# Seven-product down projection, re-shared low parts of weights and attention in pieces of one k-tile

## The chip, the cores and the metric

The kernel runs on one NeuronCore of a Trainium2 chip. The metric is the device time of one execution in microseconds. The engines are TensorE (PE in the profile; its weight loads are PEld), VectorE (DVE), ScalarE (ACT), GpSimd (POOL) and SyncE (SP, which issues most DMAs). "Low part" and "high part" are the two halves into which a float32 operand is split for an fp32r product.

## The reference

One layer of a hybrid encoder block on 512 tokens of width 1024, in float32:

```python
h = rms_norm(x, norm1_pre)
q, k, v, z, xbc, dt_raw, gates = split_cols(h @ w_in, ...)
q, k = rope(head_rms_norm(q)), rope(head_rms_norm(k))        # 8 q heads, 2 kv heads, width 64
attn_out = softmax(q k^T / 8) v @ w_attn_proj
ssd_out = ssd_branch(z, xbc, dt_raw, ...) @ w_ssd_proj       # conv, two scans, gate by silu(z)
mixed = (sigmoid(g_attn) * attn_out + sigmoid(g_ssd) * ssd_out) @ w_out
x = x + rms_norm(mixed, norm1_post)
h2 = rms_norm(x, norm2_pre)
ffn = (silu(h2 @ w_gate) * (h2 @ w_up)) @ w_down             # D_FF = 2816 = 22 k-tiles of 128
x = x + rms_norm(ffn, norm2_post)
```

## The kernel before

Every large product is made of three fp32r products (mm3, L176 to L179): low activation by high weight, high by low, high by high, accumulated in one PSUM bank of 128x512. Matrices are cut into k-tiles of 128.

Weights stream through `weights`, `wload`, `presplit` and `wnext` (L101 to L150): SP loads a raw tile, ACT casts the high part, and a letter says who makes the low part: "v" a DVE subtraction, "g" a Pool subtraction, "d" an ACT multiplication by -1 and then a DMA from Pool's queue that adds the weight from memory onto it (L145). Three buffers of raw and four each of the high and low part are in flight.

The stages come in this order. `setup` forms h transposed (hT) and q; `kvproj` makes k and v; `xbc` makes the 12 channel blocks of the conv input, on an order written out by hand for all four compute engines: after each half block the table `inner` places transposes of k, q and x, and after each block `tasks` places one step of the rope and the head norm of k and q (`krope`, `qrope`, `head_norm`). `attention` then goes over the 8 heads, with softmax rows, four transposes of 128x128 for each k-tile (L654) and, after every second head, the eight value products of both heads (L678), each 64 output rows. Its order is set by `weave`: main and fill work each yield an estimate in us, and fill (`zproj` for w_z, then `gates` for w_g) is traced when its share falls behind. Within that the scheduler of the framework orders each engine. `decays` runs in between.

The feed-forward stage has PE in an order by hand. `ffn` makes three blocks j of gate and up plainly (`prepare_plain`, slots of 512 columns with tag "t"), the first two on the first 256 tokens while the mixing steps (`combine`) of token tiles 2 and 3 still run, and the other 19 by a scheme of seven products. `down` multiplies the 22 activation tiles by w_dn in `token_major8`: all eight PSUM banks, 18 k-tiles bank by bank, the last four k-tiles by token tile so that a token tile's epilogue can start while PE works on the next. Low parts are DVE's here.

## Time and profile before

| what | value |
|---|---|
| three timed runs, median | 851.0 us (847.55 to 851.08) |
| profiled execution | 855.7 us, of it span 853.8 us |
| PE busy | 822.2 us, 4570 matmuls |
| DVE busy | 550.2 us |
| ACT busy | 434.2 us |
| POOL busy | 178.7 us |
| moved by DMA | 120.88 MB |

A busy PE is not a PE at its peak: starts of neighbouring matmuls, the list of waits and the granted clock of a stretch show where time is lost inside the busy share.

### The profile page before, as it was taken

The numbers are of one execution on the slowest core, as the hardware profiler recorded it, in microseconds if no ns is written. First come the engines' busy times: TensorE is split into PE (matmuls) and PEld (weight loads), VectorE is DVE, ScalarE is ACT, GpSimd is POOL, SyncE is SP. The second block draws the span as 40 slices with busy tenths as digits, with TensorE's granted clock in tenths as the row PEclk, the third lists the DMA queues.
The fourth block names the chain that finished last, engine by engine and source line by source line (L and its number), as shares of the span: only waits on it lengthen the run. The fifth ranks groups of instructions, "written<-read, shape, count | busy, mean of one in ns | idle before, by whom it ended". The sixth has DMA issues, their size and how long they took to land.

```text
span 853.8 us, 12071 instructions
## 1 busy us (share of the span) xinstructions
PE 822.2 (96%) x4570; PEld 689.6 (81%) x4570; DVE 550.2 (64%) x918; ACT 434.2 (51%) x775; POOL 178.7 (21%) x142
## 2 busy tenths in 40 slices
PE   8989899899899999999999989999999999999996
PEld 7768787666666777767888788999999999888885
DVE  3958884965325545676683796788788788533326
ACT  6656585554664434157333655555555556322222
POOL 3323122310113334539551011000000100000000
PEclk9989999999999999999999999999999999999999
DMA  9586551110676665137335542677666674522314
GB/s 309 173 210 146 118 142 51 50 50 0 149 175 145 162 147 137 62 111 221 124 124 196 174 124 72 183 190 196 187 186 175 174 182 151 182 94 95 99 50 148
DMA packets 42826, 120.88 MB, mean 142 GB/s; under 512 B 5264, under 2 KB 5648, under 8 KB 42768
## 3 DMA queue, kind: packets, MB, share of 16 engines
q1 hardware_dynamic: 36000, 95.46, 32.7%
q0 software_dynamic: 6768, 24.64, 16.9%
q8 instruction: 36, 0.59, 0.3%
q14 instruction: 22, 0.18, 0.1%
HBM read 111.70 MB, written 8.39 MB: 141 GB/s over the span
## 4 chain that ended last, share of the span: by engine, by line
PE 78%; DVE 9%; DMA 4%; issue 4%; ACT 3%; POOL 2%; SPq 0%; DVEq 0%; POOLq 0%; ACTq 0%
PE sa L973 10%; PE mm L177 8%; PE mm L178 8%; PE mm L179 8%; PE sc L973 6%; PE mm L973 3%; PE sb L973 3%; PE sc L177 3%; PE sc L179 3%; PE sc L178 3%; PE sa L178 2%; PE sa L179 2%; PE sa L177 2%; PE sc L678 2%; PE sb L177 2%
## 5 line engine op out<-in xcount | busy, mean ns | idle before, releaser
L142 ACT CAST whi<-raw 128x1024 fp32r<-128x1024 f32 (+3 forms) x85 | 85.0, 1003 | 56.1 <-PE sc L179 49.3
L147 POOL TENSOR_TENSOR wlo<-raw,whi 128x1024 fp32r<-128x1024 f32 (+3 forms) x31 | 65.1, 2105 | 93.5 <-ACT whi L142 91.3
L177 PE MATMUL mm<-hT,wlo 128*128 128x512 f32 x176 | 74.7, 425 | 6.5 <-DMA wlo<-in_w_xbc 4.1
L179 PE MATMUL mm<-hT,whi 128*128 128x512 f32 x176 | 70.3, 400 | 0.0
L178 PE MATMUL mm<-hT,whi 128*128 128x512 f32 x176 | 69.9, 397 | 0.0
L147 DVE TENSOR_TENSOR wlo<-raw,whi 128x1024 fp32r<-128x1024 f32 (+1 forms) x26 | 31.7, 1218 | 53.3 <-ACT whi L142 53.3
L1016 POOL DMA_DIRECT2D raw<-in_w_gu x19 | 16.4, 864 | 219.0 <-DVE wlo L1022 60.6
L1021 ACT CAST whi<-raw 128x512 fp32r<-128x512 f32 (+1 forms) x57 | 41.6, 762 | 36.3 <-PE mm L973 15.5
L1022 DVE TENSOR_TENSOR wlo<-raw,whi 128x512 fp32r<-128x512 f32 (+1 forms) x57 | 47.7, 866 | 18.5 <-ACT whi L1021 18.4
L973 PE MATMUL sa<-R,whi 128*128 128x256 f32 x304 | 56.4, 283 | 0.0
L177 PEld LDWEIGHTS mm<-hT,wlo 128*128 128x128 f32 x176 | 33.8, 192 | 17.0 <-ACT wlo L144 4.7
L973 PEld LDWEIGHTS sa<-R,whi 128*128 128x128 f32 x304 | 47.4, 192 | 0.0
L973 PE MATMUL sa<-R,wlo 128*128 128x256 f32 x152 | 43.0, 283 | 0.0
L144 ACT ACTIVATE wlo<-raw 128x1024 fp32r<-128x1024 f32 x28 | 29.7, 1060 | 25.2 <-PE mm L177 24.3
L178 PEld LDWEIGHTS mm<-hT,whi 128*128 128x128 f32 x176 | 33.8, 192 | 8.9 <-issue 2.4
L179 PEld LDWEIGHTS mm<-hT,whi 128*128 128x128 f32 x176 | 33.7, 192 | 7.8 <-issue 0.5
L145 POOL DMA_DIRECT2D wlo<-in_w_g x16 | 14.0, 872 | 108.2 <-ACT wlo L144 58.4
L639 DVE TENSOR_REDUCE nmax<-sa 128x1 f32<-128x512 f32 x32 | 21.6, 686 | 16.2 <-PE sa L637 15.9
L973 PE MATMUL sa<-h2T,b 128*128 128x256 f32 x228 | 30.5, 283 | 0.0
L1124 DVE TENSOR_TENSOR acl<-act,ach 128x512 fp32r<-128x512 f32 x22 | 14.9, 688 | 23.3 <-ACT ach L1123 23.3
L973 PEld LDWEIGHTS sa<-R,wlo 128*128 128x128 f32 x152 | 29.2, 192 | 0.1
L973 PEld LDWEIGHTS sa<-h2T,b 128*128 128x128 f32 x228 | 28.7, 192 | 0.0
(439 smaller groups left out, 2476.5 us busy)
## 6 DMA issues: line engine op xcount, KB each, us to landing
raw<-in_w_gu SPq DMA_DIRECT2D x44, 512.0 KB, 4.6
raw<-in_w_dn SPq DMA_DIRECT2D x22, 512.0 KB, 3.5
raw<-in_w_gu POOLq DMA_DIRECT2D x19, 512.0 KB, 5.3
raw<-in_w_g SPq DMA_DIRECT2D x16, 512.0 KB, 6.0
wlo<-in_w_g POOLq DMA_DIRECT2D x16, 512.0 KB, 6.7
raw<-in_w_xbc SPq DMA_DIRECT2D x12, 512.0 KB, 4.2
wlo<-in_w_xbc POOLq DMA_DIRECT2D x12, 512.0 KB, 8.0
b<-in_w_gu SPq DMA_DIRECT2D x19, 256.0 KB, 5.5
```

The costliest lines, as they stand in the source:

```text
L142: self.A.copy(h[:, :n], raw[:, :n])
L144: self.A.mul(l[:, :n], raw[:, :n], -1.0)
L147: e.tensor_tensor(l[:, :n], raw[:, :n], h[:, :n].bitcast(F32), ALU.subtract)
L177: self.T.matmul(o, ll, rh, start=first, stop=False)
L178: self.T.matmul(o, lh, rl, start=False, stop=False)
L179: self.last_mm = self.T.matmul(o, lh, rh, start=False, stop=last)
L639: V.tensor_reduce(nmax, ps, AX.X, ALU.max, negate=True)
L678: self.T.matmul(po[i * HD : i * HD + HD, :], self.vt[:, k, g * HD : g * HD + HD], pts[h - 1 + i][k], start=k == 0, stop=k == NT - 1)
L973: self.T.matmul(dst, x, y[:, k], start=start and k == 0 and i == 0, stop=k == 3 and i == 2, skip_group_check=True)
L1016: G.dma_start(p13, wgu[:, 1:3], accum_op=ALU.add)
L1021: A.copy(dst[0], src)
L1022: lo.tensor_tensor(dst[1], src, dst[0].bitcast(F32), ALU.subtract)
```

## The change

Five things change.

The down projection: the first 6 of the 22 k-tiles stay plain, the first two of them started while the last gate/up block is finished (`down_start`). The other 16 become a 2x2 block product (8 k-tiles by 256 tokens by 512 columns a block) in Strassen-Winograd form, seven products in place of eight. Sums of weight blocks are formed in memory tiles `ch` and `p3` by accumulating DMAs from Pool's queue, sums of activations by DVE, and each product's parts are added from PSUM into eight tiles `c`. PE's order by hand now covers the down projection too. New pools "la" and "lq" hold its tiles; five activation tiles move to tiles that are free by then.

Low parts of weights: kv chunks 2 and 3 from Pool to DMA, w_xbc blocks 0 to 2 from DMA to Pool, the second half of w_z from Pool to DMA.

Attention and its fill are traced in pieces of one k-tile; the value products of a k-tile are issued for both heads together, after the transposes of that k-tile.

Head norm and k: q's multiplication goes to Pool, all copies of transposed k to ACT, and the second half of k's transposes half a block later. The diagonal of row scales is made in one DVE step instead of four.

The start of the feed-forward stage: combine(2) and combine(3) are issued after the last low part of h2T; the third plain block uses tiles of 1024 columns.

The low parts on Pool's queue: before, at the kv chunks and the first blocks of w_xbc:

```order
L147 TENSOR_TENSOR wlo_367<-raw_137,whi_366 128x864
L147 TENSOR_TENSOR wlo_379<-raw_139,whi_378 128x576
L145 DMA wlo_440<-in_w_xbc 128x1024
L145 DMA wlo_447<-in_w_xbc 128x1024
L145 DMA wlo_579<-in_w_xbc 128x1024
```

after, at the same place:

```order
L147 DMA wlo_364<-in_w_kv 128x864
L147 DMA wlo_377<-in_w_kv 128x576
L149 TENSOR_TENSOR wlo_439<-raw_436,whi_438 128x1024
L149 TENSOR_TENSOR wlo_445<-raw_442,whi_444 128x1024
L149 TENSOR_TENSOR wlo_576<-raw_573,whi_575 128x1024
L147 DMA wlo_582<-in_w_xbc 128x1024
```

The kv subtractions (864 and 576 columns) have become DMAs, the first three w_xbc DMAs subtractions of 1024 columns.

PE at one group of value products (pt is a transposed probability tile, vt is v, mm the fill's bank); before, the first pair of heads:

```order
L654 MATMUL sb_1602<-cst_100,pr_1448 128x128
L678 MATMUL sc_1622<-pt_1586,vt_451 64x512
L678 MATMUL sc_1622<-pt_1479,vt_451 64x512
L678 MATMUL sc_1622<-pt_1593,vt_451 64x512
L678 MATMUL sc_1622<-pt_1486,vt_451 64x512
L678 MATMUL sc_1622<-pt_1600,vt_451 64x512
L678 MATMUL sc_1622<-pt_1493,vt_451 64x512
L678 MATMUL sc_1622<-pt_1607,vt_451 64x512
L178 MATMUL mm_1609<-wlo_1241,hT_345 128x512
L179 MATMUL mm_1609<-whi_1240,hT_345 128x512
```

after, the second pair of heads:

```order
L178 MATMUL mm_1845<-whi_1698,hT_343 128x512
L179 MATMUL mm_1845<-wlo_1699,hT_341 128x512
L180 MATMUL mm_1845<-whi_1698,hT_341 128x512
L678 MATMUL sc_1823<-pt_1746,vt_448 64x512
L678 MATMUL sc_1823<-pt_1854,vt_448 64x512
L178 MATMUL mm_1845<-whi_1705,hT_344 128x512
L179 MATMUL mm_1845<-wlo_1706,hT_342 128x512
L180 MATMUL mm_1845<-whi_1705,hT_342 128x512
L678 MATMUL sc_1823<-pt_1756,vt_448 64x512
L678 MATMUL sc_1823<-pt_1869,vt_448 64x512
L178 MATMUL mm_1845<-whi_1705,hT_344 128x512
```

Before, the products of four k-tiles stand in one row with a lone one at an end; after, two stand together for each k-tile with fill between.

DVE at the start of the feed-forward stage (L162 before and L164 after write the row scale; R and af are the mixing step's); before:

```order
L932 TENSOR_TENSOR R_1075_4537<-mm_4420,R_1074_4536 128x512
L192 RECIPROCAL ry_4521<-rt_4522 128x4
L933 SCALAR_TENSOR_TENSOR R_1074_4536<-R_1075_4537,af_4174 128x512
L206 TENSOR_TENSOR rt_4522<-ry_4521 128x4
L935 SCALAR_TENSOR_TENSOR af_4176<-R_1074_4536,af_4176 128x512
L207 TENSOR_TENSOR rt_4522<-rt_4522,rn_4520 128x4
L208 SCALAR_TENSOR_TENSOR ry_4521<-rt_4522,ry_4521 128x4
L162 COPY rstd_142<-ry_4521 128x4
L183 TENSOR_TENSOR h2T_3918<-sc_4503,h2T_3916 128x4x128
L183 TENSOR_TENSOR h2T_3919<-sc_4504,h2T_3917 128x4x128
L165 TENSOR_SCALAR diag_4530<-cst_100,rstd_142 128x128 x4
```

after:

```order
L164 COPY rstd_142<-ry_4526 128x4
L166 TENSOR_TENSOR diag_4535<-cst_100,rstd_142 128x512
L184 TENSOR_TENSOR h2T_3918<-sc_4508,h2T_3916 128x4x128
L184 TENSOR_TENSOR h2T_3919<-sc_4509,h2T_3917 128x4x128
L943 TENSOR_TENSOR R_1078_4537<-af_4174,mm_4424 128x512
L1008 TENSOR_TENSOR wlo_4684<-raw_4679,whi_4683 128x1024
```

Before, two mixing steps (L933, L935) stand between the row scale's steps, ahead of both low parts of h2T; after, the mixing steps of the last two token tiles stand behind them, and the single diagonal step ahead.

The diff, cut to its core:

```diff
-    SLOTS = {"x": 14, "z": 8, "q": 15, "t": 17, "e": 21}
+    SLOTS = {"x": 14, "z": 8, "q": 15, "t": 17, "e": 17, "a": 4}
...
-            yield a["w_kv"][:, k0 : k0 + kn, :], kn * 288, "v" if k0 == 0 else "g"
+            yield a["w_kv"][:, k0 : k0 + kn, :], kn * 288, "v" if k0 == 0 else "d"
         for j in range(12):
-            yield a["w_xbc"][j], 1024, "d"
+            yield a["w_xbc"][j], 1024, "g" if j < 3 else "d"
         for n in range(2):
             for i in range(4):
-                yield a["w_z"][n, i], 1024, "g"
+                yield a["w_z"][n, i], 1024, "gd"[n]
...
-        for t in range(NT):
-            V.tensor_scalar(diag[:, t], self.ident, dst[:, t : t + 1], None, ALU.mult)
+        V.tensor_tensor(diag, self.ident.unsqueeze(1).to_broadcast([P, NT, P]), dst.unsqueeze(2).to_broadcast([P, NT, P]), ALU.mult)
...
+        self.last_lo = self.V.tensor_tensor(lo, src, hi.bitcast(F32), ALU.subtract)
...
-        self.V.tensor_tensor(h, h, r.unsqueeze(2).to_broadcast([P, nh, HD]), ALU.mult)
+        e.tensor_tensor(h, h, r.unsqueeze(2).to_broadcast([P, nh, HD]), ALU.mult)
...
-        r = self.head_norm(*bb, NQ, self.hr[:, 8 * t : 8 * t + 8])
+        r = self.head_norm(*bb, NQ, self.hr[:, 8 * t : 8 * t + 8], self.G)
...
-                (A.copy if g else V.tensor_copy)(dst, p4[:, :, g])
+                self.A.copy(dst, p4[:, :, g])
...
-        inner = {5: ([], [kt(0)]), 6: ([kt(1)], [xt(0, 0)]), 7: ([xt(0, 1)], [xt(0, 2)]), 8: ([xt(0, 3)], []),
+        inner = {5: ([], [kt(0)]), 6: ([xt(0, 0)], [kt(1)]), 7: ([xt(0, 1)], [xt(0, 2)]), 8: ([xt(0, 3)], []),
...
-                    next(z)
+                    for _ in range(4):
+                        next(z)
...
-                    if k == 3:
-                        yield 2.6
+                    if k < KD - 1:
+                        yield 0.65
                 z = self.slot("z", [512], name="z")
                 self.A.copy(z, p)
                 self.z[t][n] = z
-                yield 2.6
+                yield 0.65
...
-    def transpose_probs(self, prs):
-        pt = []
-        for k in range(NT):
-            pp = self.ps("sb")
-            for t in range(NT):
-                self.T.transpose(pp[:, t * P : t * P + P], prs[t][:, k * P : k * P + P], self.ident)
-            d = self.slot("t", [S], name="pt")
-            (self.A.copy if k % 2 else self.V.tensor_copy)(d, pp)
-            pt.append(d)
-        return pt
+    def transpose_probs(self, prs, k):
+        pp = self.ps("sb")
+        for t in range(NT):
+            self.last_tr = self.T.transpose(pp[:, t * P : t * P + P], prs[t][:, k * P : k * P + P], self.ident)
+        d = self.slot("t", [S], name="pt")
+        (self.A.copy if k % 2 else self.V.tensor_copy)(d, pp)
+        return d
     def attention(self, decays):
         self.aT = []
-        prs, pts = {0: self.softmax_rows(0)}, {}
+        prs = {0: self.softmax_rows(0)}
         for h in range(NQ):
             if h + 1 < NQ:
                 prs[h + 1] = self.softmax_rows(h + 1)
             if h in (1, 3):
                 with self.tc.issue_after(self.last_score.ins):
                     next(decays)
-            yield 1.7
-            pts[h] = self.transpose_probs(prs.pop(h))
             yield 1.8
+            if h % 2 == 0:
+                pts = [[], []]
+            else:
+                po = self.ps("sc")
+            def weighted(k):
+                for i in range(2):
+                    g = (h - 1 + i) // (NQ // NKV)
+                    with self.tc.issue_after(self.last_tr.ins):
+                        self.T.matmul(po[i * HD : i * HD + HD, :], self.vt[:, k, g * HD : g * HD + HD], pts[i][k],
+                                      start=k == 0, stop=k == NT - 1)
+            for k in range(NT):
+                pts[h % 2].append(self.transpose_probs(prs[h], k))
+                yield 0.45
+                if h % 2 and k:
+                    weighted(k - 1)
+                    yield 0.85
+            del prs[h]
             if h % 2:
-                po = self.ps("sc")
-                for k in range(NT):
-                    for i in range(2):
-                        g = (h - 1 + i) // (NQ // NKV)
-                        self.T.matmul(po[i * HD : i * HD + HD, :], self.vt[:, k, g * HD : g * HD + HD], pts[h - 1 + i][k],
-                                      start=k == 0, stop=k == NT - 1)
+                weighted(NT - 1)
                 hi, lo = self.slot("q", [S], F32R, "aTh"), self.slot("q", [S], F32R, "aTl")
                 self.hilo(hi, lo, po)
                 self.aT.append((hi, lo))
-                yield 3.7
+                yield 0.85
...
-            self.chan_major(p, wh, wl, self.hT)
+            for k in range(KD):
+                self.chan_major(p, wh, wl, self.hT, ks=[k], first=k == 0, last=k == KD - 1)
+                if k < KD - 1:
+                    yield 0.65
             self.g_d[j] = self.spill(p)
-            yield 5.2
+            yield 0.65
...
+            if wide:
+                for i, names in enumerate((("B11", "B12"), ("B22", "B21"))):
+                    hl = [self.wp.tile([P, 1024], F32R, tag=s, name=self.nm(s), bufs=4) for s in ("whi", "wlo")]
+                    A.copy(hl[0], raw[i])
+                    V.tensor_tensor(hl[1], raw[i], hl[0].bitcast(F32), ALU.subtract)
+                    for c, n in enumerate(names):
+                        w[n] = [x[:, c * 512 : c * 512 + 512] for x in hl]
+                return w
...
-        for t in (2, 3):
-            combine(t)
+        with self.tc.issue_after(self.last_lo.ins):
+            for t in (2, 3):
+                combine(t)
...
+    def mm3f(self, o, a, b, start=False):
+        for i, (x, y) in enumerate(((a[1], b[0]), (a[0], b[1]), (a[0], b[0]))):
+            self.T.matmul(o, x, y, start=start and i == 0, stop=i == 2, skip_group_check=True)
+    def plain(self, k, t, n):
+        ah, al, (wh, wl) = self.ops[k]
+        tok, c = slice(t * P, t * P + P), slice(n * 512, n * 512 + 512)
+        self.mm3f(self.bank[t, n], (ah[:, tok], al[:, tok]), (wh[:, c], wl[:, c]), k == 0)
+    def down_operands(self, k, pool=None):
+        ah, al = (pool.tile([P, S], F32R, tag="pa", name=self.nm("pa"), bufs=6) if pool else self.slot("a", [S], F32R, "pa")
+                  for _ in range(2))
+        self.hilo(ah, al, self.act[k])
+        self.ops.append((ah, al, self.wnext()))
+    def down_start(self, late):
+        self.wseq = ((self.a["w_dn"][j], 1024, "v") for j in range(NF - 2 * PAIRS))
+        self.bank, self.ops = {}, []
+        for k in range(2):
+            self.down_operands(k)
+        for tag, n, ts in (("sc", 0, (2, 3)), ("sb", 0, (0, 1)), ("mm", 1, (0, 1)), ("sa", 1, (2, 3))):
+            for t in ts:
+                self.bank[t, n] = self.ps(tag)
+                for k in range(2):
+                    self.plain(k, t, n)
+                if late:
+                    late = late()
+    def down(self, pool):
...
+        for k in range(1, n0):
+            if k > 1:
+                self.down_operands(k, pool)
+                if k < n0 - 2:
+                    for t, n in bank:
+                        plain(k, t, n)
+            if k == 1:
+                gain = [new("gn", [512], 2) for _ in range(2)]
+                for i in range(2):
+                    self.load(gain[i], self.a["norm2_post"][i * 512 : i * 512 + 512].partition_broadcast(P))
+            if k >= 2 and k - 2 < NG2:
+                self.load(chain[k - 2], blk(k - 2, 0, 0))
+        for t, n in reversed(bank):
+            for k in (n0 - 2, n0 - 1):
+                plain(k, t, n)
...
+        def wsplit(src):
+            h, l = (self.wp.tile([P, 1024], F32R, tag=s, name=self.nm(s), bufs=4) for s in ("whi", "wlo"))
+            src = src.rearrange("p k c -> p (k c)")
+            A.copy(h, src)
+            V.tensor_tensor(l, src, h.bitcast(F32), ALU.subtract)
+            return h, l
+        def asplit(src):
+            t = splits.pop(0) if splits else new("as", [2, 256], 10, F32R)
+            A.copy(t[:, 0], src)
+            V.tensor_tensor(t[:, 1], src, t[:, 0].bitcast(F32), ALU.subtract)
+            return t[:, 0], t[:, 1]
...
+        def product(dst, b, a, start, after=None, sums=None, by_token=None, then=None):
+            kept = []
+            def prep(g):
+                w = wsplit(b(g))
+                for i in range(2):
+                    kept.append((asplit(a(2 * g + i)), [y[:, i * 512 : i * 512 + 512] for y in w]))
+                if after:
+                    G.dma_start(chain[g], after(g), accum_op=ALU.add)
+            def work(g):
+                for k in (2 * g, 2 * g + 1):
+                    x, wi = kept[k]
+                    for t in range(1 if by_token else 2):
+                        mm3(dst[t], [y[:, t * P : t * P + P] for y in x], wi, start and k == 0)
+                    if sums:
+                        sums(k)
+                if g == NG2 - 1:
+                    if by_token:
+                        by_token()
+                        for x, wi in kept:
+                            mm3(dst[1], [y[:, P : 2 * P] for y in x], wi)
+                    if then:
+                        then()
+            stages.extend((lambda g=g: prep(g), lambda g=g: work(g)) for g in range(NG2))
...
+        def sums6():
+            for t in range(2):
+                c[2 + t, 0] = cs.pop()
+                A.copy(c[2 + t, 0], u[t])
+                add(2 + t, 1, u[t], ALU.subtract)
+                add(t, 1, u[t], ALU.subtract)
+                add(2 + t, 0, x[t])
+                begin(2 + t)
...
+        def last(t):
+            add(t, 0, y[t - 2])
+            finish(t)
+        between = {4: lambda: begin(0), 5: lambda: begin(1), 6: lambda: finish(0), 7: lambda: finish(1)}
+        product(u, lambda g: chain[g], a11, True, lambda g: blk(g, 0, 1),
+                lambda k: V.tensor_tensor(r1[k], a22(k), a21(k), ALU.subtract), then=third_weights)
+        product(v, lambda g: raw(g, 1, 0), a12, False, None, lambda k: V.tensor_tensor(a21(k), a11(k), a21(k), ALU.subtract),
+                then=sums2)
+        product(a, lambda g: chain[g], lambda k: r1[k], True, lambda g: blk(g, 1, 1),
+                lambda k: V.scalar_tensor_tensor(r1[k], r1[k], -1.0, a11(k), ALU.mult, ALU.subtract), then=lambda: second(a))
+        product(x, lambda g: p3[g], a21, True, None,
+                lambda k: V.scalar_tensor_tensor(a12(k), r1[k], -1.0, a12(k), ALU.mult, ALU.subtract), then=lambda: second(x))
+        product(u, lambda g: chain[g], lambda k: r1[k], False, lambda g: blk(g, 1, 0), then=sums6)
+        product(a, lambda g: raw(g, 1, 1), a12, False, then=sums3)
+        product(y, lambda g: chain[g], a22, False, None, lambda k: between.get(k, int)(), lambda: last(2))
+        stages[0][0]()
+        for i, (_, work) in enumerate(stages):
+            if i + 1 < len(stages):
+                stages[i + 1][0]()
+            work()
+        last(3)
```

## Rows read from the trace of the kernel before

**Rows 1.** The page, span and busy time of PE.
```profile
span 853.8 us, 12071 instructions
...
PE 822.2 (96%) x4570; PEld 689.6 (81%) x4570; DVE 550.2 (64%) x918; ACT 434.2 (51%) x775; POOL 178.7 (21%) x142
```

**Rows 2.** Timeline of PE at its end: start, length (us), engine, line, operation.
```profile
845.68 0.39 PE L177 MATMUL sc<-whi,acl 128*128 128x512 f32 x1
845.91 0.39 PE L178 MATMUL sc<-wlo,ach 128*128 128x512 f32 x1
846.14 0.39 PE L179 MATMUL sc<-whi,ach 128*128 128x512 f32 x1
```

**Rows 3.** Waits of PE, whole span: us in total, times, longest us.
```profile
PE mm L177 <- DMA wlo<-in_w_xbc: 4.1, 2, 3.6
PE sb L654 <- ACT pt L656: 3.2, 1, 3.2
PE sb L372 <- ACT kT L447: 2.7, 1, 2.7
PE mm L177 <- DMA wlo<-in_w_g: 2.4, 1, 2.4
PE sa L178 <- DVE h2T L183: 1.9, 1, 1.9
PE sa L177 <- DVE pl L994: 1.5, 1, 1.5
...
PE sa L286 <- DVE diag L165: 1.3, 1, 1.3
...
PE sb L177 <- DVE hT L183: 0.7, 1, 0.7
```

**Rows 4.** Busy by stretch: PE, PEld, DVE, ACT, POOL; PEclk, DMA share, GB/s.
```profile
50.00:70.00 20.00, 16.41 (x61) 12.95 (x60) 11.82 (x25) 9.96 (x13) 4.68 (x7) 0.83 0.77 187
90.00:100.00 10.00, 7.35 (x33) 5.85 (x32) 8.70 (x17) 4.40 (x8) 0.88 (x1) 0.83 0.48 105
160.00:180.00 20.00, 16.82 (x65) 9.72 (x64) 13.36 (x26) 8.85 (x17) 9.68 (x4) 0.91 0.23 79
510.00:520.00 10.00, 10.00 (x69) 9.52 (x68) 7.90 (x12) 5.47 (x8) 2.89 (x2) 0.84 0.01 2
740.00:750.00 10.00, 10.00 (x45) 8.26 (x45) 2.87 (x4) 3.11 (x4) 0.00 (x0) 1.00 0.31 107
```

**Rows 5.** DVE by line and form: count, busy us, mean ns, idle before.
```profile
L147 DVE TENSOR_TENSOR wlo<-raw,whi 128x1024 fp32r<-128x1024 f32 x25 | 30.6, 1225 | 53.3 <-ACT whi L142 53.3
...
L1124 DVE TENSOR_TENSOR acl<-act,ach 128x512 fp32r<-128x512 f32 x22 | 14.9, 688 | 23.3 <-ACT ach L1123 23.3
...
L1099 DVE TENSOR_TENSOR g<-g,sa 128x256 f32<-128x256 f32 x19 | 7.9, 416 | 1.6 <-PE sa L973 1.1 <-ACT g L1098 0.5
```

**Rows 6.** Timeline of DVE at 30, 162 and 523 us.
```profile
29.94 4.38 DVE L183 TENSOR_TENSOR hT<-h,hT 128x512 fp32r<-128x512 f32 x2
...
161.94 0.28 DVE L514 CAST stl<-ones 128x128 fp32r<-128x128 f32 x1
...
162.43 2.48 DVE L515 CAST stl<-ones 128x128 fp32r<-128x128 f32 x1
...
523.01 2.49 DVE L994 TENSOR_TENSOR pl<-raw,ph 128x512 fp32r<-128x512 f32 x4
```

**Rows 7.** Timeline of POOL at 162 us.
```profile
162.13 4.95 POOL L147 TENSOR_TENSOR wlo<-raw,whi 128x1024 fp32r<-128x1024 f32 x2 [26.04 <-ACT whi L142]
```

**Rows 8.** Timeline of PE at two groups of value products (L678).
```profile
162.02 1.07 PE L678 MATMUL sc<-pt,vt 128*64 128x512 f32 x2
163.02 0.50 PE L177 MATMUL mm<-whi,hT 128*128 128x512 f32 x1
...
193.59 3.65 PE L678 MATMUL sc<-pt,vt 128*64 128x512 f32 x16
197.17 0.50 PE L177 MATMUL mm<-whi,hT 128*128 128x512 f32 x1
```

**Rows 9.** DMA issues by line: count, KB each, median us to landing.
```profile
wlo<-in_w_xbc POOLq DMA_DIRECT2D x12, 512.0 KB, 8.0
```

More of the change, by code (lines that the diff above doesn't have):

```diff
@@ L42 @@
 R_DTB, R_AL, R_D, R_QK, R_END = 0, 32, 64, 80, 336
+PAIRS = 8
 NPLAIN = 3
@@ L403, in kvproj @@
                 w.append((h[:, k * 288 : k * 288 + 288], l[:, k * 288 : k * 288 + 288]))
-        self.vt = self.const([P, NT, NKV * HD], name="vt")
+        self.vt = self.cp.tile([P, NT, NKV * HD], F32, tag="vt", name=self.nm("vt"))
         self.dtr = self.const([P, NT, 32], name="dtr")
@@ L515, in decays @@
             V.tensor_copy(st[:, :, :, o + 1], one)
-        self.lT = self.const([P, NT, P], F32R, "lT")
-        self.rT = self.const([P, NT, P], F32R, "rT")
+        self.lT, self.rT = (self.cp.tile([P, NT, P], F32R, tag=n, name=self.nm(n)) for n in ("lT", "rT"))
         yield
@@ L1038, in ffn @@
         rb = late = None
+        spare = [self.cp.tile([P, S], F32, tag=tag, name=self.nm("act")) for tag in ("lT", "rT", "vt")]
+        spare += [self.tp.tile([P, S], F32, tag="spill", name=self.nm("act"), bufs=2) for _ in range(2)]
         def activate(j, up, sign, g):
@@ L1109, in ffn @@
             late = (j, w, u, x7, pw, g)
-        finish(*late)
-    def down(self):
-        V, A = self.V, self.A
-        g = self.gain("norm2_post", "e")
-        self.wseq = ((self.a["w_dn"][j], 1024, "v") for j in range(NF))
-        split = {}
-        def lhs(k):
-            for i in range(k // 2 * 2, min(k // 2 * 2 + 4, NF), 2):
-                if i not in split:
-                    split[i] = hi, lo = [self.sp.tile([P, 2, S], F32R, tag="R", name=self.nm(n), bufs=8) for n in ("ach", "acl")]
-                    for e in range(2):
-                        A.copy(hi[:, e], self.act[i + e])
-                        V.tensor_tensor(lo[:, e], self.act[i + e], hi[:, e].bitcast(F32), ALU.subtract)
-            return [h[:, k % 2] for h in split[k // 2 * 2]]
-        def epilogue(t, po):
-            x = [self.slot("e", [512], name="x2") for _ in range(2)]
+        return lambda: finish(*late)
@@ new lines, in down, with blk, raw, add @@
+    def down(self, pool):
+        V, A, G, T = self.V, self.A, self.G, self.T
+        n0, wd, act = NF - 2 * PAIRS, self.a["w_dn"], self.act
+        NG2 = PAIRS // 2
+        new = lambda tag, shape, bufs, dt=F32: pool.tile([P] + shape, dt, tag=tag, name=self.nm(tag), bufs=bufs)
+        chain = [new("ch", [2, 512], NG2) for _ in range(NG2)]
+        p3 = [new("p3", [2, 512], NG2) for _ in range(NG2)]
+        r1 = [new("r1", [256], PAIRS) for _ in range(PAIRS)]
+        splits = [new("as", [2, 256], 10, F32R) for _ in range(10)]
+        cs = [new("c", [512], 8) for _ in range(8)]
+        def blk(g, k, n):
+            j = n0 + k * PAIRS + 2 * g
+            return wd[j : j + 2, :, n * 512 : n * 512 + 512].rearrange("k p c -> p k c")
+        mm3, plain, bank = self.mm3f, self.plain, self.bank
+        for k in range(1, n0):
[13 more added lines that the diff above has]
+                plain(k, t, n)
+        c = {(t, 1): cs.pop() for t in (2, 3, 0, 1)}
+        for (t, n), x in c.items():
+            A.copy(x, bank[t, n])
+        def wsplit(src):
[9 more added lines that the diff above has]
+            return t[:, 0], t[:, 1]
+        def raw(g, k, n):
+            t = self.wp.tile([P, 1024], F32, tag="raw", name=self.nm("raw")).rearrange("p (k c) -> p k c", k=2)
+            self.load(t, blk(g, k, n))
+            return t
+        lo, hi = slice(0, 256), slice(256, S)
+        a11, a12 = (lambda k: act[n0 + k][:, lo]), (lambda k: act[n0 + PAIRS + k][:, lo])
+        a21, a22 = (lambda k: act[n0 + k][:, hi]), (lambda k: act[n0 + PAIRS + k][:, hi])
+        stages = []
+        def product(dst, b, a, start, after=None, sums=None, by_token=None, then=None):
[21 more added lines that the diff above has]
+            stages.extend((lambda g=g: prep(g), lambda g=g: work(g)) for g in range(NG2))
+        def add(t, n, p, op=ALU.add):
+            V.tensor_tensor(c[t, n], c[t, n], p, op)
+        half = {}
+        def begin(t):
+            x = [new("x2", [512], 4) if t < 2 else self.slot("a", [512], name="x2") for _ in range(2)]
@@ new lines, in down, with third_weights, sums2 @@
+        u = [self.ps("sa") for _ in range(2)]
+        a = [self.ps("mm") for _ in range(2)]
+        x = [self.ps("sb") for _ in range(2)]
+        v, y = [bank[t, 0] for t in (0, 1)], [bank[t, 0] for t in (2, 3)]
+        def third_weights():
+            for g in range(NG2):
+                self.load(p3[g], blk(g, 0, 1))
+                G.dma_start(p3[g], blk(g, 1, 1), accum_op=ALU.add)
+        def sums2():
+            for t in range(2):
+                c[t, 0] = cs.pop()
+                A.copy(c[t, 0], v[t])
+                add(t, 0, u[t])
@@ new lines, in second, with sums3 @@
+        def second(p):
+            for t in range(2):
+                add(2 + t, 1, p[t], ALU.subtract)
+        def sums6():
+            for t in range(2):
+                c[2 + t, 0] = cs.pop()
[4 more added lines that the diff above has]
+                begin(2 + t)
+        def sums3():
+            for t in range(2):
+                add(t, 1, a[t], ALU.subtract)
```

52 lines of the change are left out of this document (29 added, 23 removed).

## The prediction

> **What bounds the kernel now.** I read the page first. TensorE (PE) is busy 822.2 of 853.8 us [rows 1]; so PE's own stream is the path, and two things can shorten it: fewer matmul columns, or fewer stops. The reader should take the price of a column from the end of the stream: 128x512 matmuls start 0.23 us apart (845.68, 845.91, 846.14 [rows 2]), and in a stretch without a gap 45 records fall in 10 us (740 to 750 [rows 4]), 0.222 each; I use 0.227 us. Then I read PE's list of waits for the stops: the largest seven that the change can touch sum to 4.1 + 3.2 + 2.7 + 2.4 + 1.9 + 1.5 + 1.3 = 17.1 us [rows 3]. Last I read the stretches around them for what a stop does to the clock: after each long stop the granted clock falls from the 2.4 to the 1.2 GHz level for a few us, so its mean is 0.83 over the 20 us from 50, 0.83 over 90 to 100, 0.91 over the 20 us from 160 and 0.84 over 510 to 520 [rows 4]; at 740 to 750, far from any stop, it is 1.00. Missing clock times length is what PE lost there on top of the wait: 3.4, 1.7, 1.8 and 1.6 us, less about 0.4 of the first that fell into the wait itself. So a wait costs about one and a half times its row.
>
> The profiled execution took 855.7 us (span 853.8 and 1.9 around it), 4.7 over the median 851.0 of the three timed runs. I make the sum on the profiled execution and take it off the median.
>
> **The change part by part.**
>
> *Down projection.* Before: 22 k-tiles x 4 token tiles x 2 halves x 3 = 528 matmuls of 512 columns. After: 6 k-tiles plain, 144, and seven products of 8 k-tiles x 2 token tiles x 3 = 336, together 480. 48 x 0.227 = -10.9 us, all of it on the path since PE has no gap there (10.00 busy of 10 [rows 4]).
>
> What must hide under the 336 matmuls (76 us) is new DVE work. Weights: 28 low parts of 128x1024 at 1.225 = 34. Activations and their sums: 56 + 32 pieces of 128x256 at 0.416 = 37. Adds from PSUM, gains and final steps: about 32 of 128x512 at 0.69 = 22 [rows 5]. That is 93 us by the mean durations; back-to-back runs are shorter (four of 128x512 in 2.49 us, 0.62 each [rows 6]), which scales to about 84. Some of it can run ahead under the plain matmuls, where DVE was busy 2.87 of 10 us [rows 4]: the order puts the first 10 activation splits, four weight splits (four buffers) and the 16 sums of the first two products there, 10 x 0.416 + 4 x 1.225 + 16 x 0.416 = 16 us. So DVE needs 68 to 77 us under 76: nearly the bound, but not over it. The tight place is from the fifth to the seventh product: six adds and the beginning of two epilogues stand in DVE's order ahead of the last product's weight splits, and its first pass uses all four of them in 24 matmuls, 5.4 us, while four splits take 4.9. I take +3 us, bounds 0 (all hidden) and +9 (the top of the range, 93 - 16 = 77, plus an exposed six adds and four splits, 4 + 5, at that one place).
>
> The 16 accumulating DMAs that build block sums of w_dn go through Pool's queue. The nearest row is the same kind of DMA for other weights: 8.0 us to landing [rows 9]. A chain buffer is read by the first, third, fifth and seventh product, so one whole product (10.9 us) lies between a buffer's last split and its next use: hidden, cost 0.
>
> *Tail.* Before, from the last matmul's start at 846.14 [rows 2] to the end of the span at 853.8 pass 7.7 us. After, a PSUM add (0.69) comes ahead of the squares and token tile 2's finish stands in front of tile 3's on DVE (two steps of 128x512, 1.4 [rows 5]), of which about half overlaps with ACT's square: +1.2, bounds 0 and +2.5.
>
> *Conv-input weights (w_xbc).* The first three low parts move from ACT-plus-DMA to a Pool subtraction; each needs only the cast. The two waits for such a DMA (4.1 [rows 3]) and the half clock after them (3.0 [rows 4]) are 7.1 us. Pool takes about 2.5 for one (4.95 for two [rows 7]) against the 8.0 of the DMA [rows 9]. I take -6.5, bounds -7.1 and 0. The kv chunks 2 and 3 go the other way, onto the DMA; their matmuls come at about 36 us and the landing at 37 to 38 by 8.0 from an issue near 29.5, but the Pool subtractions for these chunks, beside which DVE's hT was slow (4.38 us for two steps [rows 6], against 1.38 at 0.69 each) is gone, and with it a wait of 0.7 [rows 3]. Net +0.5, bounds -0.7 and +2.
>
> *k transposed.* PE waits 2.7 us for ACT's copies, which themselves stood behind DVE's [rows 3]; now all eight are ACT's and the second half comes half a block later. With the half clock 4.4 us. DVE, 8.70 busy of 10 from 90 [rows 4], also loses q's four multiplies to Pool. I take -3.5, bounds -4.4 and 0.
>
> *Attention.* The 3.2 us wait at 165 is a chain: Pool's two w_z subtractions from 162.13 take 4.95 us [rows 7], and under them a DVE copy of a size that takes 0.28 just before, at 161.94, takes 2.48, and the step behind it is as late [rows 6]; the copies of the transposed probabilities stand behind. The second half of w_z now goes by DMA, so the Pool work is gone from there: wait 3.2 plus half clock 1.8 = 5.0. What is late next could be that DMA: ACT's second pass and 8.0 to landing. I take -4, bounds -5 and 0.
>
> Value products: a lone one takes 1.00 us (162.02 to 163.02), eight side by side 3.58 (193.59 to 197.17), 0.45 each [rows 8]. By the order, lone ones go from six to two, -4 x 0.55 = -2.2. But visits of PE to this form go from 7 to 16. The first 512-column matmul after a visit takes 0.50 where 0.39 is usual [rows 2, 8], and as much is lost going in by the same row's measure: 9 x 0.2 = +1.8. Net -0.4, bounds -2.2 and +1.8. The Trainium skill, "TensorEngine Tiling (Array Packing)", Key Properties, says that changing the tiling mode drains TensorE, which speaks against splitting the value products into more visits; the 0.50 agrees with it, and by the rule alone this part would be a loss of 1.8.
>
> *FFN start.* The h2T low part (wait 1.9) stood on DVE behind the mixing step of tile 2; that step is now issued after it. The half clock after it is 1.6, and the third plain block's wait for "pl" (1.5) came from too few slots; it gets wide tiles instead. Sum 5.0. DVE still does the same work, so some will reappear at the next block: -4, bounds -5 and -1.5.
>
> *Diagonal in one step* instead of four: wait 1.3 goes: -1.3, bound 0. The wait for w_g (2.4) has no edit: 0.
>
> Sum: -10.9 + 3 + 1.2 - 6.5 + 0.5 - 3.5 - 4 - 0.4 - 4 - 1.3 = -25.9. 855.7 - 25.9 = 829.8 for the profiled execution, 851.0 - 25.9 = 825.1 for the median.
>
> **Rivals.**
>
> *A: DVE becomes the bound of the seven products.* For: 93 us by mean durations under 76, 16 ahead. Against: back-to-back durations. The stop then comes at nearly every product and the clock falls with it as at 57 us; +9 in place of +3 and half of that again for the clock: 825 + 6 + 4 = 835.
>
> *B: Pool's new work holds DVE.* Three w_xbc subtractions (2.5 each) and four q multiplies (about 1.3, half the columns) now run beside DVE, 12.7 us. A DVE step took 2.48 instead of 0.28 under Pool's [rows 6, 7]; if DVE is held the whole time, hT's low parts, the conv sums and k's split come late, and new stops stand where the old ones were: the 6.5 and 3.5 do not come, and part of the 1.3. 825 + 11 = 836. Against: from 50 to 70 DVE is only 11.82 of 20 busy [rows 4]. The Trainium skill, "SBUF — State Buffer", Who interferes with whom, calls this port pair an exclusive lock that a Pool instruction keeps to its end; the 2.48 us step agrees with it, and by that rule this rival is what the change would bring.
>
> *C: slower.* Each of the 12 chain accumulations lands too late. Each must beat 10.9 us and the 2.7 us (12 matmuls) of the pair of k-tiles before its use, 13.6; the saving of 25.9 is used up from 12 x 2.2 us, a landing of 15.8. Were it 17, 12 x 3.4 = 41: 825 + 41 = 866. Against: 8.0 is the longest median of such a DMA there [rows 9].
>
> *D: all stops go and nothing new comes.* -10.9 + 0 - 7.1 - 0.7 - 4.4 - 5 - 2.2 - 5 - 1.3 = -36.6: 814.
>
> **How the numbers follow.** Forecast 0.60 (its own range 819 to 831), A 0.15, B 0.13, D 0.09, C 0.03. Within 0.5% (4.3 us, about what a measurement can tell from no change) needs A and B together with little of the rest: part of C's and B's, 0.02. Faster 0.95, slower 0.03. The range takes in the forecast, D's end and A and B: 814 to 837.
>
> **What would show it.** Right: 48 fewer 512-column matmuls at 0.227 and PE busy 10 of 10 through the seven products; no PE wait for a w_xbc low part, for kT or for pt; granted clock 1.00 from 50 to 70 and 160 to 180; h2T's low part waited for under 1 us. Wrong: PE waits for DVE's weight splits or for "as" tiles in several products (A); DVE steps over 2 us beside Pool from 36 to 60 (B); PE waiting behind accumulating DMAs (C); clock dips in new places, from the kv or the w_z DMA.

## The result and the profile after

The changed kernel takes 830.5 us (830.25 to 831.16) against 851.0: ratio 0.977, interval 0.9745 to 0.9795, so 20.5 us faster. Forecast were 825 and a gain of 25.9. The profiled execution went from 855.7 to 830.4, that is 25.3 less: as a sum over the profile the forecast was 0.6 off, as a time of the median run it was 5.4 off.

The page and PE's list of waits after, to be laid beside [rows 1] and [rows 3] (columns as there):

```profile
span 828.2 us, 12216 instructions
...
PE 804.3 (97%) x4522; PEld 673.4 (81%) x4522; DVE 577.9 (70%) x999; ACT 467.3 (56%) x841; POOL 195.4 (24%) x162
```

```profile
PE sb L179 <- DMA wlo<-in_w_kv: 3.4, 1, 3.4
PE sc L829 <- DVE E L782: 3.2, 4, 0.8
PE mm L179 <- DMA wlo<-in_w_z: 2.0, 1, 2.0
...
PE sa L179 <- DVE h2T L184: 0.3, 1, 0.3
```

48 matmuls fewer; of the waits in [rows 3] none is left over 0.3 us, not even the one for w_g (2.4), which no edit was meant to touch, but three new ones are there: a kv low part, the second half of w_z, and the decay factor E of the scan stage. The windows of after (columns as in [rows 4]):

```profile
50.00:70.00 20.00, 20.00 (x90) 16.55 (x89) 13.68 (x27) 12.79 (x15) 6.71 (x9) 1.00 0.75 175
160.00:180.00 20.00, 17.97 (x95) 12.96 (x91) 12.59 (x29) 12.13 (x27) 1.70 (x2) 1.00 0.66 144
710.00:818.00 108.00, 107.90 (x478) 89.07 (x476) 87.11 (x169) 64.56 (x116) 19.25 (x16) 1.00 0.75 187
```

From 50 to 70 us, in the conv stage, PE runs through with the clock at 1.00, and it has no gap in the whole down projection although DVE is busy 87.11 of 108 us.

Where the time went, by the start of each stage's first matmul in the two traces (us, and the term of the prediction):

| stage | before | after | change | forecast |
|---|---|---|---|---|
| first product, to the diagonal | 19.35 | 17.55 | -1.8 | -1.3 |
| q, k, v | 21.43 | 25.14 | +3.7 | +0.5 |
| conv, to k's transposes | 39.47 | 32.67 | -6.8 | -6.5 |
| k's transposes to the scores | 57.67 | 53.13 | -4.5 | -3.5 |
| attention | 103.16 | 98.11 | -5.1 | -4.4 |
| scan | 123.52 | 127.53 | +4.0 | 0 |
| attention projection | 30.07 | 27.88 | -2.2 | 0 |
| feed-forward start | 48.37 | 43.50 | -4.9 | -4 |
| down | 118.29 | 107.36 | -10.9 | -10.9 + 3 |
| last matmul to the end of the span | 7.7 | 10.7 | +3.0 | +1.2 |

The rest (setup, output projections and the seven products of gate and up) is within 0.3 us a stage. Scan and attention projection belong together: some transposes and products that came behind the first matmul of the projection before come ahead of it after. From the first scan product to the end of the projection PE does the same 688 matmuls in both, in 153.6 us before and 155.4 after, +1.8.

### The profile page after: what moved, and what is told of

Read it like the earlier page. It is cut to its first block, busy times and chain, and to the rows that moved or that the text cites. A ratio compares the mean times of both kernels' runs of the same rounds, so it can differ in the third digit from the quotient of the medians.

```text
span 828.2 us, 12216 instructions
## 1 busy us (share of the span) xinstructions
PE 804.3 (97%) x4522; PEld 673.4 (81%) x4522; DVE 577.9 (70%) x999; ACT 467.3 (56%) x841; POOL 195.4 (24%) x162
## 4 chain that ended last, share of the span: by engine, by line
PE 85%; DVE 5%; DMA 4%; ACT 3%; issue 2%; POOL 1%; SPq 0%; DVEq 0%; ACTq 0%; POOLq 0%
PE sa L986 10%; PE mm L178 8%; PE mm L179 8%; PE mm L180 8%; PE sc L986 7%; PE mm L1139 4%; PE sb L1139 4%; PE sa L1139 4%; PE mm L986 3%; PE sb L986 3%; PE sc L178 3%; PE sc L180 3%; PE sc L179 3%; PE sc L678 2%; PE sc L829 2%
## 5 line engine op out<-in xcount | busy, mean ns | idle before, releaser
L144 ACT CAST whi<-raw 128x1024 fp32r<-128x1024 f32 (+3 forms) x69 | 68.1, 991 | 18.3 <-issue 10.4
L178 PE MATMUL mm<-hT,wlo 128*128 128x512 f32 x176 | 78.2, 445 | 0.0
L149 POOL TENSOR_TENSOR wlo<-raw,whi 128x1024 fp32r<-128x1024 f32 (+1 forms) x28 | 58.1, 2078 | 58.8 <-ACT whi L144 56.0
L146 ACT ACTIVATE wlo<-raw 128x1024 fp32r<-128x1024 f32 (+2 forms) x31 | 32.4, 1046 | 26.8 <-PE mm L178 23.5
L639 DVE TENSOR_REDUCE nmax<-sa 128x1 f32<-128x512 f32 x32 | 21.7, 687 | 18.3 <-PE sa L637 17.7
L1210 DVE TENSOR_TENSOR wlo<-ch,whi 128x1024 fp32r<-128x1024 f32 x16 | 19.5, 1225 | 13.7 <-ACT whi L1209 13.6
L642 ACT ACTIVATE pr<-sa,nmax 128x512 f32<-128x512 f32 x32 | 22.0, 689 | 12.4 <-DVE nmax L639 8.6
```

What stands on the lines that cost most here:

```text
L144: self.A.copy(h[:, :n], raw[:, :n])
L146: self.A.mul(l[:, :n], raw[:, :n], -1.0)
L149: e.tensor_tensor(l[:, :n], raw[:, :n], h[:, :n].bitcast(F32), ALU.subtract)
L178: self.T.matmul(o, ll, rh, start=first, stop=False)
L639: V.tensor_reduce(nmax, ps, AX.X, ALU.max, negate=True)
L642: self.last_exp = A.activation(pr, ps, AF.Exp, bias=nmax, accum_out=sm)
```

## The experiments

Times are medians of four runs unless said; "changed" is 830.5. Before itself had medians of 848.5, 852.5 and 850.2 us beside the three sets of experiments, and a fall of the clock for 3.4 us costs up to 1.7 us; so differences of 1 or 2 us are judged by the stages and waits of the profiles.

**The kernel before, once more.** No edit.

> The kernel before, unchanged, for a second profile. Its first profiled execution took 855.7 us, its timed runs 847.6 to 851.1. Theory (the prediction's transfer): the profile shows the typical run and profiling adds the 4.7 us; then this profile takes 855 to 856 us with the same list of waits. Rival: the stops of before vary from execution to execution; then this one takes 847 to 852 us, and some of the waits (w_xbc 4.1, pt 3.2, kT 2.7, w_g 2.4, h2T 1.9, pl 1.5) or half-clock stretches are missing or shorter.

This profile took 852.4 us. The list of waits is that of [rows 3] within 1.1 us a row, but low clock is missing at two places: from 8.1 us for 3.4, in the first product, and at the feed-forward start:

```profile
50.00:70.00 20.00, 16.12 (x60) 12.74 (x59) 11.62 (x24) 9.62 (x11) 4.45 (x7) 0.83 0.76 184
510.00:520.00 10.00, 9.15 (x72) 8.47 (x70) 7.78 (x11) 7.94 (x13) 2.93 (x2) 1.00 0.01 2
```

PEclk at 510 is 1.00 where [rows 4] has 0.84; that stage took 46.28 us against 48.37. The 21 timed runs of before beside the experiments went from 846.5 to 855.1, and their mean granted clock went with them: on one chip 0.994 at 846.5 to 848.5, 0.988 at 851.5, 0.986 at 853.7. So the waits recur, the clock's fall after one does not always, and the first profile (mean clock 0.986) was an execution with many falls: two falls of 3.4 us at half clock are 3.4 us, and the two profiles are 3.3 apart. The rival holds in kind; its number (847 to 852) was just missed.

**Whole fill in the scan stage.** In effect:

```diff
-            for k in range(KD):
-                self.chan_major(p, wh, wl, self.hT, ks=[k], first=k == 0, last=k == KD - 1)
+            self.chan_major(p, wh, wl, self.hT)        # w_g in the scan stage alone
```

> The changed kernel, but in the scan stage the w_g fill is traced in whole blocks of 24 matmuls as before; attention keeps its pieces of one k-tile. In the changed kernel the scan stage has 36 visits to fill instead of 19 and took 4.0 us longer. Theory: the visits cost it (17 more, about 0.2 us each, and four waits of 0.8 for the decay factor E that short pieces no longer cover); undone, 830.5 falls by 3.5 to 4.5 to 826 to 827, and the waits for E are gone. Rival: the scan stage is longer because DVE and Pool are busier or come later there; then 830 to 831, and the waits for E stay.

828.4, 2.1 less, where the theory had 3.5 to 4.5. The waits for E are gone, as it says, and the scan stage is back at 123.87 (from 127.53). But 1.1 of these 3.7 us only moved behind the stage's end: the attention projection takes 28.94 instead of 27.88. Both together take 152.8 instead of 155.4, so the pieces cost 2.6 there. PE's list of waits for this stretch has 3.4 us in the changed kernel, 3.2 of it for E, and 1.2 here. That is 2.2 of the 2.6, and 0.4 is left for 17 visits, 0.02 each: the waits for E cost it, and the visits next to nothing. The clock moved too, without much effect on the sum: in this profile it fell after the w_z wait (from 174.1 us for 3.4; first value product to scan 2.1 longer) and not after the kv wait (q, k, v 1.8 shorter).

**kv low parts on Pool again.**

```diff
-"v" if k0 == 0 else "d"
+"v" if k0 == 0 else "g"
```

> The changed kernel with the low parts of kv chunks 2 and 3 back on Pool. Theory: the DMA is late (PE waits 3.4 us for it, then 1.5 us of half clock), and Pool was in time at the price of 0.7 to 0.9 for hT's low part: 830.5 falls by 3.5 to 4.5 to 826 to 827. Rival: with w_xbc's first subtractions behind them on the same engine, Pool now becomes late for w_xbc, and DVE is held longer: 829 to 834, with a wait for a w_xbc or hT low part.

829.9, 0.6 less: the rival's number and its wait. The kv wait is gone and hT's low part is waited for instead; DVE (timeline) is held by Pool:

```profile
27.83 2.91 DVE L149 TENSOR_TENSOR wlo<-raw,whi 128x864 fp32r<-128x864 f32 x1
30.66 2.49 DVE L184 TENSOR_TENSOR hT<-h,hT 128x512 fp32r<-128x512 f32 x2
```

```profile
PE sb L178 <- DVE hT L184: 2.3, 2, 1.4
```

The 864 columns take 1.05 us in the trace of the changed kernel. The q, k, v stage is 2.6 shorter all the same (22.59 for 25.14); what hides it in this profile is a fall of the clock after the w_z wait (from 174.2 for 3.4), which the changed kernel's profile has not. So the new wait took back only part of the theory's gain.

**w_z's second half on Pool again.**

```diff
-yield a["w_z"][n, i], 1024, "gd"[n]
+yield a["w_z"][n, i], 1024, "gg"[n]
```

> The changed kernel with the second half of w_z back on Pool; the pieces of one k-tile stay. Theory: Pool's subtractions hold DVE in the attention stage as before, so the wait for pt and the half clock come back (5.0 us in the profile of before) against the 2.2 us wait for the w_z DMA that goes: 833 to 834. Rival: the pieces alone cover that stop, and the DMA only costs: 828 to 829, with no wait for pt.

838.2, 7.7 more, over twice the theory's loss. Three Pool subtractions take 7.20 us, three DVE steps of 128x128 under them 2.4 to 2.5 each, and now the value products, pinned behind the transposes in PE's order, wait too; the clock is low from 160.8 us for 6.8:

```profile
PE sc L678 <- DVE pt L654: 6.3, 1, 6.3
```

```profile
153.81 7.20 POOL L149 TENSOR_TENSOR wlo<-raw,whi 128x1024 fp32r<-128x1024 f32 x3 [26.93 <-ACT whi L144]
153.98 2.38 DVE L504 TENSOR_TENSOR dk<-dk 128x128 f32<-128x128 f32 x1 [0.31 <-ACT dec L503]
156.28 2.53 DVE L513 TENSOR_TENSOR str<-dk,str 128x128 fp32r<-128x128 f32 x1
158.73 2.42 DVE L514 CAST str<-ones 128x128 fp32r<-128x128 f32 x1
```

**w_xbc's first low parts by DMA again, alone, and together with kv on Pool.**

```diff
-yield a["w_xbc"][j], 1024, "g" if j < 3 else "d"
+yield a["w_xbc"][j], 1024, "d"
```

> The changed kernel with the first three w_xbc low parts back on the DMA; the kv chunks stay on theirs. Theory: the late DMA is what the conv stage lost before, so the 6.8 us of that stage come back (a wait of 3 to 4 us and up to two low-clock stretches at 1.7 each), minus what the wait for kv already lets the DMAs catch up: 835 to 837, with PE waiting for a w_xbc low part. Rival: the gain of that stage came from DVE's lighter load; then 830 to 831 and no such wait.

831.6, 1.1 more: the theory fell. The conv stage takes 32.67 us, as in the changed kernel, without a wait for w_xbc. The second kernel undoes both letters:

> The changed kernel with both letters as before: kv chunks 2 and 3 on Pool and the first w_xbc low parts by DMA. Each alone as before took 829.9 and 831.6, with no wait for w_xbc. Theory: either edit is enough, because Pool's kv subtractions hold DVE's hT steps, and those put ACT's half of the w_xbc low parts and so their DMA late; with both undone the wait of 3 to 4 us and the low clock behind it are back, 834 to 837. Rival: the single diagonal step, 1.8 us earlier, is what brought the DMA in time; then 828 to 830 and no such wait.

```profile
PE mm L178 <- DMA wlo<-in_w_xbc: 4.1, 1, 4.1
```

The conv stage is back at 39.60 in its profile (836.8 us), while either edit alone leaves it at 32.7 (32.68 with kv on Pool). So in the profiles either edit does it, as the theory has it. The timelines give the reason: the DMA for w_xbc is issued when ACT's half is done, and that stands behind the hT casts that wait for DVE.

```profile
34.38 1.95 ACT L183 CAST hT<-h 128x512 fp32r<-128x512 f32 x3 [2.87 <-DVE h L294]
46.73 0.86 POOL L147 DMA_DIRECT2D wlo<-in_w_xbc  x1 [6.84 <-ACT wlo L146]
```

With kv by DMA that issue was at 43.18. In time the theory's 834 to 837 did not come: the four runs go from 829.2 (mean clock 0.997) to 836.8 (0.991) with median 831.7, and the profiled one is the slowest. How often the full loss comes is not settled by one trace.

**Value products of a head pair together, behind the last transposes.**

```diff
-                if h % 2 and k:
-                    weighted(k - 1)
...
-                weighted(NT - 1)
+                for k in range(NT):
+                    weighted(k)
```

> The changed kernel, but the eight value products of a head pair stand together behind the last transposes, so PE visits that form 4 times instead of 16; all else stays in pieces of one k-tile. Theory of the prediction: a visit costs about 0.2 us, so 12 fewer give 2.4 us: 828. Rival: the pieces hide the copies of the transposed probabilities, and together they wait for the last copy, four times 0.5 to 1 us: 830.5 to 832, with a wait of L678 for pt.

825.8, 4.6 less, and its profile shows no wait for pt: the rival fell, and the gain is about twice the theory's. On the kernel of three mends below it was tried again:

> The kernel of three mends with the value products of a head pair together. Theory: the 12 visits fewer are worth the same here as in the changed kernel (4.7 us, 0.39 a visit), since no stop lies between: 820.7 - 4.7 = 816. Rival: part of that difference came from the other stop in the attention stage, which the mends have removed: 818 to 820.

817.3, 3.4 less than that kernel, between the theory's 816 and the rival's 818; in the profile the attention stage takes 91.2 us instead of 95.8, 4.5 less. That is 0.38 for each of 12 visits, not 0.2; but two lone products went with them, which take 1.00 each where two side by side take 0.895. Without these (2 x 0.45) it is 0.3 a visit. PE's timeline in the changed kernel shows what a visit is made of:

```profile
202.48 0.40 PE L180 MATMUL mm<-whi,hT 128*128 128x512 f32 x1
202.81 1.08 PE L678 MATMUL sc<-pt,vt 128*64 128x512 f32 x4
203.81 0.50 PE L178 MATMUL mm<-whi,hT 128*128 128x512 f32 x1
204.15 0.40 PE L179 MATMUL mm<-wlo,hT 128*128 128x512 f32 x1
```

0.33 and 0.34 where 0.227 is usual, and two products in 1.00 where [rows 8] give 0.895 for two of eight in a row: 0.1 each time, 0.3 in all, the same.

**Three mends.** Whole fill in the scan stage, and

```diff
-"v" if k0 == 0 else "d"
+"d" if k0 == 6 else "v"
-"gd"[n]
+("gggg", "dddv")[n][i]
```

> The changed kernel with three mends: whole fill in the scan stage, kv chunk 2 (k-tiles 3 to 5) as a DVE subtraction and chunk 3 by DMA, and the last k-tile pair of w_z's second half as a DVE subtraction. Theory: each removes a stop seen in the profile (3.7, 3.4 and 2.0 to 2.5 us, and the low clock after the latter two): 830.5 - 8 to 11 = 820 to 823. Rival: DVE, held by Pool's subtraction at 34.6 us and 77% busy from 30 to 50 us, is late for hT instead, and only the scan stage's gain is left: 826 to 828.

820.7, 9.8 less. By stages it is 4.5 in q, k, v, 2.4 in attention and 2.9 in scan and attention projection; the two weight mends were not run apart. No PE wait is over 1.1 us and the granted clock stays at the 2.4 GHz level from 10.5 us to the end of the matmuls; four runs lie within 1.3 us. With the value products together, 817.3 (816.6 to 817.7; ratio to before 0.961, interval 0.957 to 0.965) is the fastest kernel of this study.

**Part of two epilogues earlier**, on the kernel of three mends:

```diff
                 add(t, 0, u[t])
+                early[t] = self.tiny(2, "ss")
+                self.square_sum(early[t][:, 1:2], c[t, 0], self.rstd[:, t : t + 1])
+                V.tensor_tensor(c[t, 0], c[t, 0], gain[0], ALU.mult)
```

> As the kernel of three mends, and in the down projection the first half of token tiles 0 and 1 is squared and multiplied by its gain right after the second product, where DVE has room, and not in the last one. Theory: after the last matmul 10.7 us pass since DVE still has token tile 2's end before it; two multiplications of 0.6 fewer there and the same chain behind them shorten the tail by 1 to 2 us: 1 to 2 us below the kernel of three mends. Rival: the tail is bound by the chain of small steps of tiles 2 and 3, which stay: no difference.

822.4, 1.7 more, neither theory. The tail is 0.7 shorter (10.02 for 10.75), but the down stage takes 109.65 instead of 107.39, with three PE waits that the kernel of three mends does not have:

```profile
PE mm L1144 <- DVE wlo L1215: 0.7, 1, 0.7
PE sc L1144 <- DVE as L1221: 0.7, 2, 0.5
```

So DVE is within a us or two of being the bound there.

**The mixing steps not held back**: combine(2) and combine(3) without issue_after.

> The changed kernel without holding combine(2) and combine(3) back behind the last low part of h2T. The feed-forward start (from the first h2T matmul to the first of the seven products) takes 43.5 us now, 48.4 and 46.3 in two profiles of before, the latter without low clock. Theory: the order of DVE is what removed the wait of 1.4 to 1.9 and the wide tiles the 1.5: 831.5 to 833, a wait for h2T's low part of 1 to 2 us. Rival: the new wide tiles are all of it: 830 to 831.

833.2, 2.7 more. The wait for h2T's low part is 1.4, as the theory says:

```profile
PE sa L179 <- DVE h2T L184: 1.4, 1, 1.4
...
PE sc L1138 <- DVE as L1215: 0.7, 2, 0.5
...
PE mm L1138 <- DVE wlo L1209: 0.5, 1, 0.5
```

The feed-forward start takes 44.55 instead of 43.50, so of the gain there (2.8 us against the second profile of before, without low clock) the order brought 1.0. The rest is about the wait for "pl" (1.5) that the wide tiles were to remove; no run has them undone alone. The other 2.1 us of loss are in the down stage (109.43), with PE waits for DVE of 1.2 in all; why that stage too is touched, the runs do not show.

**Half the pairs**: PAIRS = 4, 14 plain k-tiles, the epilogue steps at k = 0 to 3 of the last product.

> The changed kernel with 14 plain k-tiles and 8 in the seven products in place of 6 and 16: 504 matmuls instead of 480 in the down projection. Theory: matmuls set its time and DVE is hidden: 24 x 0.227 = 5.4 more to the last matmul; the tail of 10.7 us stays, being a chain of steps and not a backlog: 836. Rival: the tail is DVE's backlog of the seven products and shrinks with half of them by 1 to 2: 834 to 835.

838.7, 8.2 more. To the last matmul the stage takes 6.1 more for 24 matmuls (5.4 by 0.227, and 0.3 is a new wait for DVE), 0.25 each, so matmuls set its time, at a little over the price used; the tail grew from 10.7 to 12.8. It is a backlog, but the other way round than the rival had it: the last product is half as long and hides less of the epilogues.

## Why the prediction was right or wrong

That the sum comes out 0.6 from the profile (25.9 for 25.3) is luck in good part. By the table kv, the scan stage and the tail cost 9.0 us more than forecast, and the other seven terms brought 8.6 more. The gains for k, the diagonal and the wide tiles rest on the table and on waits that are gone; no run undoes these edits alone.

*The down term* was right: -10.93 for -10.9. The +3 for stops was too much: there were none. The count of DVE work was about right (87 us busy), and the last experiments show how near the edge it is. Rival A did not come, but its reason, DVE close to its bound, stands.

*The tail* was mis-sized, +3.0 for +1.2, beyond its bound of 2.5. The step that failed is "about half overlaps": only tile 2 was seen in front of tile 3. DVE's timeline around the last matmul (817.51):

```profile
815.80 2.73 DVE L1284 SCALAR_TENSOR_TENSOR c<-c,ry,x 128x512 f32<-128x512 f32 x4
818.46 0.21 DVE L1280 TENSOR_SCALAR rv<-ss 128x1 f32<-128x1 f32 x1
...
820.12 1.42 DVE L1284 SCALAR_TENSOR_TENSOR c<-c,ry,x 128x512 f32<-128x512 f32 x2
821.46 0.68 DVE L1278 TENSOR_TENSOR c<-c,gn 128x512 f32<-128x512 f32 x1
...
823.43 1.42 DVE L1284 SCALAR_TENSOR_TENSOR c<-c,ry,x 128x512 f32<-128x512 f32 x2
```

Token tiles 0 and 1, which the term left out, end only at 818.5; then comes all of tile 2, and only then tile 3.

*w_xbc*: -6.8 for -6.5, but put down to one edit where either does it. I gave the gain to the subtraction on Pool; by the profiles taking kv off Pool does the same, because it frees DVE. The row of the slow hT steps [rows 6] was read only for its 0.7 us wait and not for what stood behind it on ACT.

*kv*: +3.7 for +0.5, beyond the bound of 2. The step "landing at 37 to 38 by 8.0 from an issue near 29.5" failed: the issue was at 30.8 (Pool's DMA instructions alone take 0.9 to 1.0), the landing took 8.8, and the fall of the clock behind the wait (from 40.1 us for 3.4) was not priced at all, though "clock dips in new places" was a sign that the prediction named.

```profile
30.80 1.93 POOL L147 DMA_DIRECT2D wlo<-in_w_kv  x2 [3.31 <-ACT wlo L146]
```

```profile
39.74 0.37 PE L179 MATMUL sb<-wlo,hT 128*128 128x288 f32 x1 [3.36 <-DMA wlo<-in_w_kv]
```

*k transposed* (-4.5 for -3.5), *the diagonal* (-1.8 for -1.3), *attention* (-5.1 for -4.4) and *the feed-forward start* (-4.9 for -4) came out near the sum. For the diagonal that says little: the first product's stage takes from 16.7 to 18.3 us in the profiles that share this code, and before's profile had a fall of the clock in it; what is shown is that the wait for diag is gone. Of the feed-forward start, 2.1 us were in the first profile of before alone (48.37, and 46.28 in the second). In attention errors offset each other. The stop for pt and its low clock went whole (4.9 for 4). The wait for w_g, which was priced at 0, went too (2.4), and no run shows by which edit; one of 2.0 for the w_z DMA came. The visits cost about 0.3 x 9 = 2.7 instead of 1.8. The Trainium skill's rule that a change of tiling mode drains TensorE ("TensorEngine Tiling (Array Packing)", Key Properties) would have made this part a loss: by the price that the runs gave it was one, of 0.5 us (2.7 less the 2.2 of the lone products). The traces agree: without waits and low clock the attention stage takes 95.3 us before and 95.9 after.

*The scan stage* was missing from the sum: +4.0, or +1.8 together with the attention projection. The diff traces the w_g fill in pieces of one k-tile, and I followed that only through attention. In the scan stage PE goes to the fill 36 times instead of 19. What this costs is not the visits: the short pieces no longer cover four waits for E (3.2 us), as the second experiment shows. A timeline can mislead here:

```profile
238.26 1.02 PE L740 MATMUL sb<-xw,Bt 128*128 128x512 f32 x2
238.72 0.80 PE L178 MATMUL mm<-hT,wlo 128*128 128x512 f32 x1
239.36 0.40 PE L179 MATMUL mm<-hT,whi 128*128 128x512 f32 x1
```

The first fill matmul behind the float32 product stands 0.64 ahead of the next where 0.23 is usual. But the product's two records start 0.43 apart and the fill is stamped only 0.03 behind the second. From 238.26 to 239.36 pass 1.10 us, which is 2 x 0.43 and 0.23: nothing is lost.

*The attention projection*'s -2.2 was not in the sum either. 1.1 of it is the scan stage's, by the second experiment (28.94 with the whole fill, 28.9 to 29.0 in all four kernels that have it); about 1 is in the first profile of before alone (30.07, and 29.12 in the second).

*Rival B* was right that Pool holds DVE: wherever kv or w_z were on it (the third and fourth experiment), and under the first w_xbc subtraction of the changed kernel too. There three steps take 4.22 us that take 2.07 with w_xbc by DMA:

```profile
34.59 4.22 DVE L294 SCALAR_TENSOR_TENSOR h<-xT,gcol,rbs 128x512 f32<-128x512 f32 x3
```

No wait of PE for hT is in the changed kernel's list (the kv wait may hide one), and the losses that the rival counted did not come. The Trainium skill's exclusive lock ("SBUF — State Buffer", Who interferes with whom) agrees with 2.91 instead of 1.05 us and with the 2.4 to 2.5 us steps.

*The transfer to the median* is the step that made the time too low. As a sum over the profile it holds, 25.9 for 25.3. But the profile of before had 20.4 us of low clock ahead of its last matmul, the one of after 3.4; at half clock that is 8.5 of the 25.3. By the first experiment their number varies from run to run, so the median run of before most likely had fewer of them to lose. I saw that the profile was 4.7 over the median and assumed that this would stay.

## What to carry to other kernels

Where PE is full, follow a finer piece through every stage that it reaches: in attention each visit to the 64-row products cost about 0.3 us, and in the scan stage the visits cost next to nothing, but the short pieces left waits of 0.8 uncovered. Before a long step in a timeline is called a loss, add up the starts over the whole group. Price the first stop in a chain of stops and follow what stands behind it on every engine before giving a gain to one edit. If a profiled execution is slower than its median, compare the granted clocks first, since what they cost cannot be gained twice.

## What the runs showed of the hardware

A wait of PE of 2 to 4 us is followed by a fall of the granted clock to the 1.2 GHz level in some executions and not in others. After the same w_z wait of 1.9 to 2.5 us it fell in five of these profiles and not in three; it stayed low for 3.4 us there, which is 1.7 us of loss. After the kv wait of 3.4 to 3.6 us it fell in three and not in one, and after the w_g wait of 2.4 to 2.5 us in neither profile of before, so "after each long stop" in the prediction says too much. The spread of before (846.5 to 855.1) and of the kernel with both letters undone (829.2 to 836.8) goes with it; the kernel of three mends, without such waits, spreads over 1.3 us.
